# Token gather of a mixture-of-experts kernel: two expert units served by one float32r gather in two parts

## The chip, the cores and the metric

The kernel runs on one core of a Trainium2 chip, in one launch. Its time is the device time in microseconds: three runs gave 1655.13, 1655.5 and 1658.3 us, the median is 1655.5 us. The profile is of one further execution.

## The reference

Two layers, each a token mixer and then a mixture of experts (MoE), on 256 tokens of 1024 channels, all float32. The change lies in the MoE:

```
scores = sigmoid(xf @ w_router)                  # 64 experts
idx    = top 8 of the experts in the 4 best of 8 groups, by scores + b_router
w      = scores[idx] / (sum + 1e-20) * 2.5
y[t]   = sum over the 8 experts e of token t:  w[t,e] * swiglu(x[t], w1[e], w3[e], w2[e])
shared = swiglu(x, ws1, ws3, ws2)
x      = x + g_f * (y + shared)
# swiglu(x, w1, w3, w2) = (silu(x @ w1) * (x @ w3)) @ w2 ; w1, w3: 1024x256, w2: 256x1024
```

Every expert's three matrices (3 MB) are used by every execution, so each layer reads 201 MB of expert weights.

## The kernel before

Names: PE is TensorE (PEld its weight loads), DVE VectorE, ACT ScalarE, SP SyncE, which issues all weight DMAs (SPq in the profile).

**Units.** `moe_body` (L1366) runs 27 units per layer (`UNITS`, L58 to L67): units of 2 experts with 64 token slots each, of 4 experts with 32 slots, and four of 1 expert with 128 slots. The first three units hold the six experts with fixed numbers; the others are sorted by load, so their weights are found by numbers that the routing computes (`ids`, read into registers by SP, L246).

**One unit** (loop at L1613), in PE's order, which is written out by hand:
- `psT<-w,xe`: the up projection. `xe` is the unit's input (128 slots, 1024 channels), w a tile of `w13`.
- `psG<-posTi,identb` and `psG<-wg,oh`: token positions and weights of the slots; DVE makes from them `oT` (scatter one-hots) and `gt`, and `hh`, the gated product (L1626 to L1637).
- `psA<-oT,Y`: `combine` (L1605) scatters the unit before into the accumulators, 16 float32r products of 128x128 by 256 columns.
- two transposes of `hh`, then ACT copies them to `hT_` (L1653).
- `gather(u + 1, 0)`: 4 channel blocks of the next unit's input, `ht` (the tokens, float32) times the one-hot `oh` of 128 columns, two token tiles each.
- `psS<-w,hT_`: `lower` (L1659), the down projection, in two halves; ACT and DVE write `Y` and its remainder (`weigh`, L1675).
- `gather(u + 1, 1)`: the other 4 channel blocks. DVE copies the first half to `xe`, ACT the second.

A float32 product is two instructions on PE, a float32r product one. DVE builds `oh` of the next unit after `gt` (L1579).

**Weights.** `Stream` (L105) issues the loads in the order of use. Tiles are 2 MB; there are nine slots, five named `w` in a ring and four named `wx`, dealt out by `PATTERN` (L70). A unit of 2 experts takes three tiles, of 4 experts six, of 1 expert one and a half. SP waits for a slot to be free, then issues; a slot is free when PE has read its tile for the last time. Loads of experts beyond the first six wait for the routing.

**Routing.** Ahead of the units, `h` is transposed into `ht` (`h_tok`, L1374), DVE computes the routing (L1455 to L1543), and PE fills its waits with the shared expert (`up`, `down`). `gather(0, ...)` follows.

Of the kernel before, what the change touches and what calls it, by code (L numbers as in the profile page):

```python
# [11 lines left out]
F32 = mybir.dt.float32  # L12
F32R = mybir.dt.float32r
BF16 = mybir.dt.bfloat16
I32 = mybir.dt.int32
AF = mybir.ActivationFunctionType
OP = mybir.AluOpType
# [4 lines left out]
P = 128  # L22
D = 1024
KC = D // P
S = 256
NT = S // P
# [35 lines left out]
UNITS = list(_F)  # L62
# [4 lines left out]
NU = len(UNITS)  # L67
# [63 lines left out]

# what a mixer keeps in the extra weight slots until it has no more use for it (tag, floats, buffers)
ROOMS = ((("hp", 1144, 1), ("e0", 385, 1), ("e1", 385, 1), ("e2", 385, 1), ("e3", 385, 1),
# [6 lines left out]
class Shared:  # L140
    """A pool of which some tags lie in the extra weight slots."""

# [26 lines left out]
def trunk(ctx, tc, A, out, dbg=None):  # L169
    nc = tc.nc  # L170
# [20 lines left out]
    def bank(tag):  # L191
        if tag == "S":
            turn[0] ^= 1
            tag = f"S{turn[0]}"
        return ps.tile([P, 512], F32, name="ps" + tag, tag=tag, bufs=4 if tag == "A" else 1)

    def mm(o, lhsT, rhs, start=True, stop=True):
        pe.matmul(out=o, lhsT=lhsT, rhs=rhs, start=start, stop=stop, skip_group_check=True)  # L198

    # ---------------------------------------------------------------- weights  # L200
    st = Stream()
# [112 lines left out]

    # ---------------------------------------------------------------- constants
    tcol = [const.tile([P, NCOL], F32, name=f"tcol{l}") for l in range(L)]
# [124 lines left out]

    # ---------------------------------------------------------------- helpers
    def rsqrt(pool, ss, scale, tags=None, out=None, gap=None):
# [47 lines left out]
    def c2(ap, n=2):  # L491
        return ap.rearrange("p (c t) -> p c t", c=n)

    # ---------------------------------------------------------------- vectors
    modv = [const.tile([P, 48], F32, name=f"modv{l}") for l in range(L)]
# [18 lines left out]

    # ---------------------------------------------------------------- modulation
    mod_ready = set()
# [25 lines left out]

    # ---------------------------------------------------------------- norm
    def chan_sum(b, x, w, first, last):
# [36 lines left out]

    # ---------------------------------------------------------------- mixer
    def mixer(l, before):
# [7 lines left out]
    def mixer_body(l, pool, before=None):  # L591
# [15 lines left out]

        # weights: split into a rounded part and its remainder, ahead of their products
        seq = []
# [113 lines left out]

        # modulation vectors, a few vector operations at a time
        def mod_fill():
# [17 lines left out]

        # convolution
        hp = pool.tile([P, 4, S + 30], F32, name="hp")
# [73 lines left out]

        # rotary embedding and per-head norms  # L820
        def rot(raw):
# [50 lines left out]

        # differential attention
        def a_head(hd):
# [113 lines left out]

        # stick-breaking attention
        def c_head(hd):  # L990
# [100 lines left out]
        def quads(ns):  # L1091
# [5 lines left out]
            if l == 0:  # L1097
                # the first half of the channels in plain float32, ahead of the second half's modulation
                for n in ns:
                    w = wget(("in", n)).rearrange("p (j f) -> p j f", j=KC)  # L1100
                    for c in range(4):
                        for j in range(4):
                            mm(out(n, c), w[:, j, c * P:(c + 1) * P], early[j], start=j == 0 and c % 2 == 0, stop=False)
                second()
# [246 lines left out]

    # ---------------------------------------------------------------- moe
    wscaled = {}
# [12 lines left out]
    def moe_body(l, pool, sums):  # L1366
        st.open.update((l, k) for k in range(NEXTRA))
        st.upto(len(st.items))
        h = pool.tile([P, KC, S], F32, name="h", tag="Y")
        ht = pool.tile([P, NT, KC, P], F32, name="ht")  # L1370
        pre = [pool.tile([P, 1024], F32, name="pre", tag="xe", bufs=2) for _ in range(2)]
        hsT = pool.tile([P, 2, S], F32, name="hsT")

        def h_tok(t, jq):  # L1374
            b = bank("A")
            for k in range(4):
                pe.transpose(out=b[:, k * P:(k + 1) * P], in_=h[:, jq * 4 + k, t * P:(t + 1) * P], identity=ident)
            src = c2(b, 4)
            se.activation(ht[:, t, jq * 4:(jq + 1) * 4], src, AF.Copy)

        with tc.manual_schedule(engines={ET.DVE, ET.Activation}):
            # norm, logits
            w2s = st.get(("s2", l))
            ws2 = w2s[:, 0:2048].rearrange("p (j f) -> p j f", j=2)
            wr = w2s[:, 2048:2048 + KC * NE].rearrange("p (j e) -> p j e", j=KC)
            sq = pre[0][:, 0:S]
            se.activation(sq, xT[:, KC - 1], AF.Square)
# [14 lines left out]
            w13s = st.get(("s13", l)).rearrange("p (j m f) -> p m j f", m=2, j=KC)  # L1402
            # shared expert, in the waits of the routing
            sil = pre[1][:, 512:1024]

# [19 lines left out]
            def some(g, n=99):  # L1425
                for _ in range(n):
                    if next(g, 1):
                        return
# [25 lines left out]

            # routing  # L1455
            bi = pool.tile([P, NT, NE], F32, name="bi", tag="oT", bufs=2)
# [37 lines left out]

            # positions, ranks, permutation
            bp = bank("T")
# [35 lines left out]
            for t in range(NT):  # L1532
                mm(bw[:, P + t * NE:P + (t + 1) * NE], wT[:, t * P:(t + 1) * P], perm)
            some(up_, UP2)
            idt = pool.tile([1, NE], I32, name="idt")
            ve.tensor_copy(idt, bq[0:1, 0:NE])
# [5 lines left out]
            wg = pool.tile([P, NT, NE], F32, name="wg")  # L1542
            ve.tensor_copy(wg, bw[:, P:P + NT * NE].rearrange("p (t e) -> p t e", t=NT))  # L1543

        def overflow_ids():
# [28 lines left out]

        # experts
        oh = {}
        xe = {}

        def onehot(u):  # L1579
            i0, n, c = UNITS[u]  # L1580
            o = oh[u] = pool.tile([P, NT, P], F32, name="oh", bufs=2)
            ve.tensor_tensor(o.rearrange("p t (i c) -> p t i c", c=c),
                             iof[:, None, None, 0:c].to_broadcast([P, NT, n, c]),
                             posI[:, :, i0:i0 + n].unsqueeze(3).to_broadcast([P, NT, n, c]), op=OP.is_equal)
            xe[u] = pool.tile([P, KC, P], F32, name="xe", bufs=2)

        def gather(u, hf):
            b = bank("G" if u else "A")
            for k in range(4):
                for t in range(NT):  # L1590
                    mm(b[:, k * P:(k + 1) * P], ht[:, t, 4 * hf + k], oh[u][:, t], start=(t == 0), stop=(t == NT - 1))
            dst = xe[u][:, 4 * hf:4 * hf + 4]
            if hf:
                se.activation(dst, c2(b, 4), AF.Copy)
            else:
                ve.tensor_copy(dst, c2(b, 4))

        onehot(0)
        for hf in range(2):
            gather(0, hf)  # L1600
        some(up_)
# [11 lines left out]
        for u, (i0, n, c) in enumerate(UNITS):  # L1613
            X = xe[u]
            b = bank("T")
            nj = KC // n
            for j in range(KC):
                if j % nj == 0:
                    wt_ = st.get(("w13", l, i0, j // nj)).rearrange("p (k j f) -> p k j f", k=n, j=nj)
                for k in range(n):  # L1620
                    mm(b[k * c:(k + 1) * c, :], X[:, j, k * c:(k + 1) * c], wt_[:, k, j % nj],
                       start=(j == 0), stop=(j == KC - 1))
# [7 lines left out]
            for t in range(NT):  # L1630
                mm(bg[:, S:S + n], oh[u][:, t], wg[:, t, i0:i0 + n], start=(t == 0), stop=(t == NT - 1))
            oT = pool.tile([P, S], F32R, name="oT", bufs=2)
# [7 lines left out]
            if u == U_OVER:  # L1640
                overflow(l, pool, r, acc, wres, ovi, st.get(("over", l)))
            nxt = u + 1 < NU
            if nxt:
                onehot(u + 1)
            if u == 0:
# [7 lines left out]
            se.activation(hT_, b[:, 0:2 * P].rearrange("p (j s) -> p j s", j=2), AF.Copy)  # L1653
            if nxt:
                gather(u + 1, 0)
            Y = pool.tile([P, 4, 512], F32R, name="Y")
# [24 lines left out]
            if u < NU - 1:  # L1681
                for hf in range(2):
                    lower(hf)
                    weigh(hf)
                if nxt:
                    gather(u + 1, 1)

        # the last unit by halves of the channels, then the residual
        sums = bank("G")
        sq = pool.tile([P, KC, S], F32, name="nsq", tag="ht")  # L1690

# [74 lines left out]

    # ---------------------------------------------------------------- program
    def opening(pool, split):
# [124 lines left out]
```

## Time and profile before

| | us |
|---|---|
| runs, median (lowest to highest) | 1655.5 (1655.13 to 1658.3) |
| the profiled execution, its span from first to last instruction | 1657.0 |
| PE busy | 1617.4 (98%) |
| DVE busy | 748.7 (45%) |
| ACT busy | 469.0 (28%) |
| DMA queue q1, share of 16 engines | 82.5% |

The page gives no time of the profiled execution beside its span; the span lies within the range of the timed runs. PE's granted clock was 0.986 of 2.4 GHz in the mean. Matmuls overlap, so that "mean ns of one" is longer than the step from one to the next; steps are read from the starts in the timeline. The units of layer 0 run from about 349 to 829 us, those of layer 1 from about 1168 to 1650 us.

### The profile page before, as it was taken

The page shows a single profiled execution, that of the slowest core. Times are in us where ns is not written, and L with a number is a line of the kernel's source. Part 1 is how long each engine was busy: PE and PEld are TensorE (multiplying, and loading weights), DVE is VectorE, ACT ScalarE, POOL GpSimd, SP SyncE. Part 2 cuts the span into 40 slices and gives each one's busy share as a digit, 9 for nine tenths or more (in the row PEclk, how much of TensorE's full clock was granted, in tenths as well). Part 3 has the DMA queues.
Part 4 walks back from the last instruction along what each step waited for, and adds up shares of the span by engine and source line. Part 5 has one row for each costly group of instructions (what it writes and reads, how often), then busy time and mean ns, then how long its engine had stood idle before and what let it go on. Part 6 is the DMA issues. An engine that isn't in the chain of part 4 may idle for free. (4 is left out here: it accounts for less than half of the span.)

```text
span 1657.0 us, 27149 instructions
## 1 busy us (share of the span) xinstructions
PE 1617.4 (98%) x10542; PEld 1132.1 (68%) x10542; DVE 748.7 (45%) x1858; ACT 469.0 (28%) x911; POOL 2.9 (0%) x26
## 2 busy tenths in 40 slices
PE   6999999999999999999989999999999999999998
PEld 5999869875555655555578888898655565555654
DVE  8799988642221221212259997554222121221122
ACT  3546724421111111111244355344011111111111
POOL 0000000000000000000000000000000000000000
PEclk9999979999999999999999999999999999999999
DMA  9885319959999999999969744246799999999997
GB/s 379 352 328 206 149 56 363 392 222 344 369 408 421 364 414 415 413 418 413 410 247 365 280 169 153 102 193 246 275 333 396 412 410 372 402 416 416 415 412 286
DMA packets 99205, 544.10 MB, mean 328 GB/s; under 512 B 11136, under 2 KB 11776, under 8 KB 56064
## 3 DMA queue, kind: packets, MB, share of 16 engines
q1 hardware_dynamic: 99072, 542.32, 82.5%
q8 instruction: 85, 1.39, 0.3%
q14 instruction: 48, 0.39, 0.1%
HBM read 541.23 MB, written 1.05 MB: 327 GB/s over the span
## 5 line engine op out<-in xcount | busy, mean ns | idle before, releaser
L1634 DVE TENSOR_SCALAR oT<-psG,slot 128x256 fp32r<-128x256 f32 x54 | 26.1, 484 | 441.9 <-PE psG L198 441.9
L198 PEld LDWEIGHTS psG<-oh,ht 128*128 128x128 f32 x1664 | 194.5, 192 | 40.6 <-DVE Y L1678 36.0
L198 PE MATMUL psT<-w,xe 128*64 128x512 f32 (+2 forms) x1152 | 217.1, 596 | 3.8 <-DMA w<-in_w_dram 3.8
L198 PE MATMUL psA<-hH,WH 128*128 128x256 f32 x696 | 210.7, 303 | 1.1 <-ACT WH L681 1.1
L198 PE MATMUL psG<-oh,ht 128*128 128x128 f32 x1664 | 207.8, 278 | 0.4 <-issue 0.2
L681 ACT ACTIVATE WH<-w 128x512 fp32r<-128x512 f32 (+2 forms) x272 | 147.8, 553 | 203.9 <-PE psA L198 187.7
L198 PE MATMUL psA<-hH,WL 128*128 128x256 f32 x696 | 198.1, 285 | 1.3 <-DVE WL L682 1.3
L198 PE MATMUL psA<-hL,WH 128*128 128x256 f32 x696 | 197.8, 284 | 0.7 <-DVE hL L570 0.7
L682 DVE TENSOR_TENSOR WL<-w,WH 128x512 fp32r<-128x512 f32 (+2 forms) x272 | 157.2, 590 | 58.5 <-ACT WH L681 57.9
L198 PE MATMUL psT<-wx,xe 128*64 128x512 f32 (+2 forms) x896 | 171.5, 594 | 0.0
L198 PEld LDWEIGHTS psT<-w,xe 128*64 128x64 f32 (+2 forms) x1152 | 67.8, 128 | 126.4 <-issue 118.2
L1678 DVE SCALAR_TENSOR_TENSOR Y<-psS,gt,Y 128x512 fp32r<-128x512 f32 x108 | 81.1, 751 | 161.1 <-ACT Y L1677 161.1
L198 PE MATMUL psA<-room,w 128*128 128x256 f32 x592 | 145.2, 389 | 1.1 <-ACT room L573 1.1
L1677 ACT ACTIVATE Y<-psS,gt 128x512 fp32r<-128x512 f32 x108 | 74.4, 689 | 234.4 <-PE psS L198 234.4
L198 PEld LDWEIGHTS psA<-hH,WH 128*128 128x128 f32 x696 | 133.3, 192 | 5.0 <-ACT WH L681 2.7
L198 PEld LDWEIGHTS psA<-hL,WH 128*128 128x128 f32 x696 | 133.3, 191 | 3.0 <-DVE hL L570 0.9
L198 PEld LDWEIGHTS psA<-hH,WL 128*128 128x128 f32 x696 | 133.1, 191 | 2.2 <-DVE WL L682 2.1
L198 PEld LDWEIGHTS psT<-wx,xe 128*64 128x64 f32 (+2 forms) x896 | 54.9, 129 | 97.8 <-issue 95.4
L198 PEld LDWEIGHTS psA<-room,w 128*128 128x128 f32 x592 | 109.6, 194 | 17.3 <-issue 2.9
L1624 ACT ACTIVATE sl<-psT 128x256 f32<-128x256 f32 x54 | 20.8, 385 | 351.9 <-PE psT L198 351.9
L198 PE MATMUL psA<-oT,Y 128*128 128x256 f32 x864 | 115.9, 286 | 0.9 <-ACT Y L1677 0.8
L525 DVE SCALAR_TENSOR_TENSOR w<-w,room 128x1024 f32<-128x1024 f32 x96 | 115.6, 1219 | 1.5 <-DMA w<-in_w_mod_dram 1.4
(576 smaller groups left out, 1885.2 us busy)
## 6 DMA issues: line engine op xcount, KB each, us to landing
w<-in_w_dram SPq DMA_DIRECT2D x108, 1024.0 KB, 15.7
w<-in_w_dram SPq DMA_DIRECT2D x192, 512.0 KB, 10.2
wx<-in_w_dram SPq DMA_DIRECT2D x92, 1024.0 KB, 13.7
wx<-in_w_dram SPq DMA_DIRECT2D x144, 512.0 KB, 10.2
w<-in_w_in_dram SPq DMA_DIRECT2D x56, 1024.0 KB, 8.6
w<-in_w_mod_dram SPq DMA_DIRECT2D x48, 1024.0 KB, 9.3
w<-in_w_out_dram SPq DMA_DIRECT2D x8, 1024.0 KB, 7.9
wx<-in_w_dram SPq DMA_DIRECT2D x4, 2048.0 KB, 16.5
```

Source lines behind the costliest of these rows:

```text
L198: pe.matmul(out=o, lhsT=lhsT, rhs=rhs, start=start, stop=stop, skip_group_check=True)
L525: ve.scalar_tensor_tensor(t[:, j], t[:, j], 1.0, crow, op0=OP.mult, op1=OP.mult, accum_out=modv[l][:, c:c + 1])
L681: se.activation(H[:, j:], src, AF.Copy)
L682: ve.tensor_tensor(Lo[:, j:], src, H[:, j:].bitcast(F32), op=OP.subtract)
L1624: se.activation(sl, b[:, 0:FF], AF.Silu)
L1634: ve.tensor_scalar(oT, bg[:, 0:S], slot[:, k_:k_ + 1], None, op0=OP.is_equal)
L1677: se.activation(Y[:, hf], b, AF.Copy, scale=gt)
L1678: ve.scalar_tensor_tensor(Y[:, 2 + hf], b, gt, Y[:, hf].bitcast(F32), op0=OP.mult, op1=OP.subtract)
```

## The change

The tokens are kept as two float32r tiles, `htH` (rounded, by ACT) and `htL` (the remainder, by DVE in `h_rest`). A one-hot `oh` now has 256 columns, for two units, and `gather(p, s, tag)` fills one input tile `xe` of 256 slots for both, in four pieces of two channel blocks; a block takes four float32r products (two token tiles, `htH` and `htL`). The pieces for the next pair stand in the second unit of a pair only; the 27th unit has a pair of its own, of 128 columns. `oh` and `xe` have one buffer in place of two. One piece of the gather uses the bank `T`. Comments are taken out, and the scratch for DMAs of GpSimd is set to 4096.

```diff
-        ht = pool.tile([P, NT, KC, P], F32, name="ht")
+        htH, htL = (pool.tile([P, NT, KC, P], F32R, name=n) for n in ("htH", "htL"))
+        rests = []
...
-            se.activation(ht[:, t, jq * 4:(jq + 1) * 4], src, AF.Copy)
+            js = slice(jq * 4, (jq + 1) * 4)
+            se.activation(htH[:, t, js], c2(b, 4), AF.Copy)
+            rests.append((htL[:, t, js], c2(b, 4), htH[:, t, js].bitcast(F32)))
+
+        def h_rest(n):
+            for _ in range(n):
+                lo, src, hi = rests.pop(0)
+                ve.tensor_tensor(lo, src, hi, op=OP.subtract)
...
+        twos = [range(u, min(u + 2, NU)) for u in range(0, NU, 2)]
+        def onehot(p):
+            w = len(twos[p]) * P
+            o = oh[p] = pool.tile([P, NT, w], F32R, name="oh")
+            for k, u in enumerate(twos[p]):
...
+            xe[p] = pool.tile([P, KC, w], F32, name="xe")
+        def gather(p, s, tag):
+            w = len(twos[p]) * P
+            m = 512 // w
+            if m * s >= KC:
+                return
+            b = bank(tag)
+            for k in range(m):
+                parts = [(t, x) for t in range(NT) for x in (htH, htL)]
+                for i, (t, x) in enumerate(parts):
+                    mm(b[:, k * w:(k + 1) * w], x[:, t, m * s + k], oh[p][:, t], start=(i == 0), stop=(i == len(parts) - 1))
+            dst = xe[p][:, m * s:m * s + m]
...
             some(up_, UP2)
+            h_rest(2)
             idt = pool.tile([1, NE], I32, name="idt")
...
+            onehot(0)
+            h_rest(2)
...
-        for hf in range(2):
-            gather(0, hf)
+        for s in range(4):
+            gather(0, s, "A")
...
+            turn_ = u == twos[p][-1] and p + 1 < len(twos)
...
-            if nxt:
-                gather(u + 1, 0)
+            if turn_:
+                gather(p + 1, 0, "G")
...
-                for hf in range(2):
-                    lower(hf)
-                    weigh(hf)
-                if nxt:
-                    gather(u + 1, 1)
+                lower(0)
+                weigh(0)
+                if turn_:
+                    gather(p + 1, 1, "G")
+                    gather(p + 1, 2, "T")
+                lower(1)
+                weigh(1)
+                if turn_:
+                    gather(p + 1, 3, "G")
```

PE in layer 0, before: the end of unit 1 (2 experts), from its scatter to the up projection of unit 2.

```order
L198 MATMUL psA<-oT,Y 128x256 x16
L1651 MATMUL psT<-ident,hh 128x128 x2
L198 MATMUL psG<-oh,ht 128x128 x8
L198 MATMUL psS_3849<-w,hT__3836 64x512 x4
L198 MATMUL psS_3850<-w,hT__3836 64x512 x4
L198 MATMUL psG<-oh,ht 128x128 x8
L198 MATMUL psT<-wx,xe 64x512 x16
```

The same place with the change, from the transposes of unit 0 (first of its pair) to the up projection of unit 2; each left-out stretch repeats the pair of `htH` and `htL` (eight products to a piece).

```order
L1668 MATMUL psT<-ident,hh 128x128 x2
L198 MATMUL psS_3744<-wx,hT__3741 64x512 x4
L198 MATMUL psS_3745<-wx,hT__3741 64x512 x4
L198 MATMUL psT<-w,xe 64x512 x16
...
L1668 MATMUL psT<-ident,hh 128x128 x2
L198 MATMUL psG<-oh,htH 128x256
L198 MATMUL psG<-oh,htL 128x256
...
L198 MATMUL psS_3852<-w,hT__3839 64x512 x4
...
L198 MATMUL psT<-oh,htL 128x256
L198 MATMUL psS_3853<-w,hT__3839 64x512 x4
...
L198 MATMUL psT<-wx,xe 64x512 x16
```

Unit 0 now goes from its transposes straight to `psS`; unit 1 gathers for units 2 and 3 in four pieces around the two halves of its `psS`.

DVE in layer 0, before: from the last of the routing to the shared expert's product `hsT`.

```order
L1525 TENSOR_SCALAR posT<-posT 64x256
L1550 SCALAR_TENSOR_TENSOR cap<-cap,cap_3951 64x1
L1551 TENSOR_SCALAR cap_3951<-rank 64x1
L1552 TENSOR_TENSOR cap<-cap,cap_3951 64x1
L1536 CAST idt<-psT 1x64
L1555 TENSOR_SCALAR wres,ov<-posT,cap 64x256
L1539 COPY posI<-psG 128x128
L1541 CAST posTi<-psT 64x256
L1543 COPY wg<-psG 128x128
L1582 TENSOR_TENSOR oh<-iof,posI 128x256 x2
L1556 TENSOR_TENSOR wres<-wres,wT 64x256
L1416 TENSOR_TENSOR hsT<-psS_3582,pre 128x512
```

The same place with the change.

```order
L1561 TENSOR_SCALAR posT<-posT 64x256
L1385 TENSOR_TENSOR htL<-psA,htH 128x512 x2
L1573 CAST idt<-psT 1x64
L1576 COPY posI<-psG 128x128
L1578 CAST posTi<-psT 64x256
L1580 COPY wg<-psG 128x128
L1396 TENSOR_TENSOR oh<-iof,posI 128x2x128 x2
L1385 TENSOR_TENSOR htL<-psA,htH 128x512 x2
L1452 TENSOR_TENSOR hsT<-psS_3582,hsT 128x512
```

Two subtractions stand ahead of `idt` (the expert numbers for SP) and two behind the one-hots; the overflow's `cap` and `wres` moved behind `hsT`.

## Rows read from the trace of the kernel before

**Rows 1.** The page, part 1: busy time, share of the span, instructions.
```profile
span 1657.0 us, 27149 instructions
PE 1617.4 (98%) x10542; PEld 1132.1 (68%) x10542; DVE 748.7 (45%) x1858; ACT 469.0 (28%) x911; POOL 2.9 (0%) x26
```
**Rows 2.** Windows: stretch, its length, busy per engine, PE clock, DMA share, GB/s.
```profile
349.30:460.00 110.70, 109.81 (x700) 64.03 (x702) 22.83 (x54) 15.09 (x28) 0.00 (x0) 1.00 0.93 353
580.00:820.00 240.00, 238.09 (x1603) 133.24 (x1599) 50.61 (x115) 38.03 (x69) 0.20 (x1) 1.00 1.02 414
1166.00:1643.00 477.00, 473.50 (x3057) 271.65 (x3055) 99.01 (x229) 72.31 (x132) 0.00 (x0) 1.00 0.99 392
1166.00:1270.00 104.00, 103.11 (x631) 60.20 (x633) 20.50 (x48) 14.32 (x26) 0.00 (x0) 1.00 0.92 343
1360.00:1390.00 30.00, 30.00 (x177) 17.53 (x178) 6.15 (x12) 5.10 (x9) 0.00 (x0) 1.00 0.95 345
1390.00:1640.00 250.00, 247.39 (x1652) 139.12 (x1648) 51.48 (x117) 38.41 (x70) 0.00 (x0) 0.99 1.02 412
```
**Rows 3.** SP's waits, 1160 to 1260 us: waiter, releaser, total, times, longest.
```profile
SPq L251 <- PE psS L198: 47.7, 5, 24.8
SPq L251 <- PE psT L198: 25.8, 9, 6.0
```
**Rows 4.** Timeline, PE, a unit: start, length, engine, operation, count, [idle before].
```profile
654.64 7.09 PE L198 MATMUL psT<-wx,xe 128*64 128x512 f32 x32
662.36 2.13 PE L198 MATMUL psA<-oT,Y 128*128 128x256 f32 x16
664.32 0.38 PE L1651 MATMUL psT<-ident,hh 128*128 128x128 f32 x2
664.54 1.95 PE L198 MATMUL psG<-oh,ht 128*128 128x128 f32 x16
666.42 3.70 PE L198 MATMUL psS<-w,hT__6091 128*64 128x512 f32 x16
670.05 2.05 PE L198 MATMUL psG<-oh,ht 128*128 128x128 f32 x16
672.03 3.65 PE L198 MATMUL psT<-w,xe 128*64 128x512 f32 x16
```
**Rows 5.** Timeline, PE and SP, the last unit and last load of either layer.
```profile
815.11 0.33 SPq L251 DMA_DIRECT2D wx<-in_w_dram  x1
824.55 1.88 PE L198 MATMUL psS<-wx,hT__7205 128*32 128x512 f32 x4
...
1630.32 4.20 SPq L251 DMA_DIRECT2D wx<-in_w_dram  x4
1643.55 1.95 PE L198 MATMUL psS<-w,hT__14033 128*32 128x512 f32 x16 [0.47 <-ACT hT__14033 L1653]
1645.29 1.88 PE L198 MATMUL psS<-wx,hT__14033 128*32 128x512 f32 x4
```
**Rows 6.** Tile `wx`, 1600 to 1657 us: from issue to landing.
```profile
DMA to landing us min/median/max: 10.2/10.3/13.8
```
**Rows 7.** Timeline: DVE beside the routing and in a unit, PE's first gather.
```profile
345.07 0.21 DVE L1536 CAST idt<-psT 1x64 int32<-1x64 f32 x1 [1.71 <-PE psT L198]
349.11 3.73 PE L198 MATMUL psA<-oh,ht 128*128 128x128 f32 x32
349.31 0.69 DVE L1416 TENSOR_TENSOR hsT<-psS,pre 128x512 f32<-128x512 f32 x1 [1.77 <-PE psS L198]
...
663.61 0.43 DVE L1582 TENSOR_TENSOR oh<-iof,posI 128x256 f32<-128x256 f32 x1
```
**Rows 8.** Timeline, PE: a unit of 1 expert after a wait for its weights.
```profile
1527.95 8.83 PE L198 MATMUL psT<-w,xe 128*128 128x512 f32 x16 [2.23 <-DMA w<-in_w_dram]
```
**Rows 9.** The clock there, in windows, columns as in rows 2.
```profile
1530.00:1540.00 10.00, 10.00 (x41) 5.82 (x40) 1.21 (x4) 0.60 (x2) 0.00 (x0) 0.90 1.00 418
```
**Rows 10.** The chain of work that ended last: start, length, engine and line.
```profile
1546.76 6.87 PE psT L198 x16
```

More of the change, by code (lines that the diff above doesn't have):

```diff
@@ L1369, in moe_body @@
         h = pool.tile([P, KC, S], F32, name="h", tag="Y")
-        ht = pool.tile([P, NT, KC, P], F32, name="ht")
-        pre = [pool.tile([P, 1024], F32, name="pre", tag="xe", bufs=2) for _ in range(2)]
+        htH, htL = (pool.tile([P, NT, KC, P], F32R, name=n) for n in ("htH", "htL"))
         hsT = pool.tile([P, 2, S], F32, name="hsT")
+        rests = []
         def h_tok(t, jq):
@@ L1377, in h_tok @@
                 pe.transpose(out=b[:, k * P:(k + 1) * P], in_=h[:, jq * 4 + k, t * P:(t + 1) * P], identity=ident)
-            src = c2(b, 4)
-            se.activation(ht[:, t, jq * 4:(jq + 1) * 4], src, AF.Copy)
+            js = slice(jq * 4, (jq + 1) * 4)
[5 more added lines that the diff above has]
+                ve.tensor_tensor(lo, src, hi, op=OP.subtract)
+        oh, xe = {}, {}
+        twos = [range(u, min(u + 2, NU)) for u in range(0, NU, 2)]
[3 more added lines that the diff above has]
+            for k, u in enumerate(twos[p]):
+                i0, n, c = UNITS[u]
+                ve.tensor_tensor(o[:, :, k * P:(k + 1) * P].rearrange("p t (i c) -> p t i c", c=c),
+                                 iof[:, None, None, 0:c].to_broadcast([P, NT, n, c]),
+                                 posI[:, :, i0:i0 + n].unsqueeze(3).to_broadcast([P, NT, n, c]), op=OP.is_equal)
+            xe[p] = pool.tile([P, KC, w], F32, name="xe")
[10 more added lines that the diff above has]
+            dst = xe[p][:, m * s:m * s + m]
+            if s % 2:
+                se.activation(dst, c2(b, m), AF.Copy)
+            else:
+                ve.tensor_copy(dst, c2(b, m))
         with tc.manual_schedule(engines={ET.DVE, ET.Activation}):
@@ L1385, in moe_body @@
             wr = w2s[:, 2048:2048 + KC * NE].rearrange("p (j e) -> p j e", j=KC)
-            sq = pre[0][:, 0:S]
+            sq = pool.tile([P, S], F32, name="pre", tag="sl", bufs=2)
             se.activation(sq, xT[:, KC - 1], AF.Square)
@@ L1402, in moe_body @@
             w13s = st.get(("s13", l)).rearrange("p (j m f) -> p m j f", m=2, j=KC)
-            sil = pre[1][:, 512:1024]
+            sil = hsT.rearrange("p c t -> p (c t)")
             def up(m):
@@ L1573, in moe_body @@
         D_(f"rank{l}", rank)
[L1576 to L1598, printed above, removed]
-        for hf in range(2):
-            gather(0, hf)
+        for s in range(4):
+            gather(0, s, "A")
         some(up_)
@@ L1613, in moe_body @@
         for u, (i0, n, c) in enumerate(UNITS):
-            X = xe[u]
+            p, off = u // 2, u % 2 * P
+            X = xe[p]
+            turn_ = u == twos[p][-1] and p + 1 < len(twos)
             b = bank("T")
@@ L1620, in moe_body @@
                 for k in range(n):
-                    mm(b[k * c:(k + 1) * c, :], X[:, j, k * c:(k + 1) * c], wt_[:, k, j % nj],
+                    mm(b[k * c:(k + 1) * c, :], X[:, j, off + k * c:off + (k + 1) * c], wt_[:, k, j % nj],
                        start=(j == 0), stop=(j == KC - 1))
@@ L1630, in moe_body @@
             for t in range(NT):
-                mm(bg[:, S:S + n], oh[u][:, t], wg[:, t, i0:i0 + n], start=(t == 0), stop=(t == NT - 1))
+                mm(bg[:, S:S + n], oh[p][:, t, off:off + P].bitcast(F32), wg[:, t, i0:i0 + n], start=(t == 0), stop=(t == NT - 1))
             oT = pool.tile([P, S], F32R, name="oT", bufs=2)
@@ L1641, in moe_body @@
                 overflow(l, pool, r, acc, wres, ovi, st.get(("over", l)))
-            nxt = u + 1 < NU
-            if nxt:
-                onehot(u + 1)
+            if turn_:
+                onehot(p + 1)
             if u == 0:
@@ L1681, in moe_body @@
             if u < NU - 1:
-                for hf in range(2):
-                    lower(hf)
-                    weigh(hf)
-                if nxt:
-                    gather(u + 1, 1)
+                lower(0)
[5 more added lines that the diff above has]
+                weigh(1)
+                if turn_:
+                    gather(p + 1, 3, "G")
         sums = bank("G")
-        sq = pool.tile([P, KC, S], F32, name="nsq", tag="ht")
+        sq = pool.tile([P, KC, S], F32, name="nsq", tag="htH")
         def residual(m):
@@ L1881 @@
     from concourse.bass_utils import run_bass_kernel_spmd as _run
-    nc = _bacc.Bacc("TRN2", target_bir_lowering=False, num_devices=1)
+    nc = _bacc.Bacc("TRN2", target_bir_lowering=False, num_devices=1, dynamic_dma_scratch_size=4096)
     arrays, args = {}, {}
```

## The prediction

> **What bounds the kernel now.** I read the page first. PE is busy 98% of the span [rows 1], which says that PE is the bound and that less work on PE is less time. That is an average, and the units need another look: the windows with the DMA rate beside PE's busy time [rows 2]. Two things are to be seen there. In the late part of both layers (580 to 820, 1390 to 1640 us) the DMAs move 414 and 412 GB/s over 250 us without a pause, while PE is busy nearly throughout: two resources are full at once. In the first 104 us of layer 1's units they move only 343, in layer 0 353, and behind the units of one expert 345. Who holds them up is told by SP's waits in the early stretch [rows 3]: for PE's reads of the weights, 47.7 us behind psS and 25.8 us behind psT. So early on the queue lacks free slots, which PE hands out; later the slots are there and the transfers themselves are the limit.
>
> How close the two are is seen at the end. The last load of layer 1 is issued at about 1634.5 us (1630.32 and 4.20) [rows 5]; such a load lands after 10.3 us [rows 6], at about 1644.8; PE takes it at 1645.29. In layer 0 it is 815.11 and 10.3, so 825.4, and PE works on it from 824.55 [rows 5]. PE finishes each layer with no margin behind the weights. A shorter PE alone then ends nothing sooner; the last byte must land sooner.
>
> **What the change takes from PE.** One unit, start to start, is 672.03 - 654.64 = 17.39 us [rows 4]. Its two gathers take 666.42 - 664.54 = 1.88 and 672.03 - 670.05 = 1.98 us, 3.86 together, so 7.72 us for a pair. With the change a pair costs 32 float32r products of 128x128 by 256 columns. The nearest row is the scatter, of the same type and shape: 16 in 664.32 - 662.36 = 1.96 us, 0.1225 us each. 32 of them are 3.92 us. Saved so far: 3.80 us a pair. Bounds for one product: half that, if only the columns counted and the scatter were held by something else, and 0.235 us, two of the steps of the present gather (1.88/16 = 0.1175). I take 0.1225, the row that is alike in everything.
>
> Two small terms go the other way. In the first unit of a pair the gather no longer stands between the transposes and psS, and covered there ACT's copy to hT_. Where no gather stands there now, in the last unit, PE waits 0.47 us for it [rows 5]. In the second unit DVE makes two one-hots, 0.43 us each [rows 7], one more than now; the present one is ready at 664.04, and the gather starts at 664.54, so 0.0 to 0.3 us of wait, the larger for units of four experts; I take 0.3. A pair then saves 3.80 - 0.47 - 0.3 = 3.03 us, a unit 1.5, and the 26 units whose successors are gathered for about 39 us a layer. The lone 27th unit has float32r products of 128 columns, for which there is no row: 32 of them at 0.06 to 0.235 us, 2 to 7.5 us against 3.86; I take 0.12 each, no change, and either end is covered by the wait for weights there.
>
> The routing gains four subtractions of 128x512 from PSUM, 0.69 us each by the row of hsT, and both pairs stand in idle time of DVE [rows 7]: two in the 1.71 us ahead of idt, where three small operations have moved away, two in the 1.77 us ahead of hsT. At zero; without the cover 2.8 us a layer, 1.4 of it ahead of idt, which the loads of the sorted experts wait for. The first gather is 32 products in either version: 3.73 us for the group now, 3.92 then, 0.2 us later.
>
> Copies to xe stay at one DVE and one ACT copy per unit in the mean. With one buffer of xe the copies must come behind the pair's last psT; they do, since the pieces stand behind it in PE's order. The third piece sits in the bank T, which the next psT needs: its DVE copy (0.69) has the whole second half of psS (half of 670.05 - 666.42, 1.8 us) and the fourth piece (1.0) to finish. The order of the loads is unchanged. Nothing here adds to PE.
>
> **What arrives at the end.** If all of it arrived, 39 us twice would be 78. It can't: from 1166 to 1643 us the core moves 477 us x 392 GB/s = 187 MB [rows 2], and at 413 GB/s these take 453 us. That floor leaves 24 us a layer. The 24 us are the stretches below the full rate. The first 104 us carry 35.7 MB, which at 413 take 86.4 us: 17.6 us lost. The stretch at 1360 carries 10.35 MB in 30 us where 25.1 would do: 4.9 us lost. The rest is crumbs.
>
> How much comes back depends on how much sooner PE frees slots. The early stretch holds six units (104/17.4), each 1.5 us shorter: 9 of the 17.6 us. The later dip arises because two units of one expert need few bytes and the queue runs full ahead of PE; with PE 1.5 us a unit faster from the start it falls behind less: 3 to 4 of the 4.9. The sum is 12.5 us a layer by which the last byte lands sooner. In both layers the end follows the last load, as shown, so the end moves by the same: 25 us in all. Off go 0.2 us twice for the first gather, and a little for a slow clock: PE will now wait, and after the one long wait of the present trace, 2.23 us, the same 16 instructions took 8.83 us [rows 8] in place of 6.87 [rows 10], with a granted clock of 0.90 of 2.4 GHz in that window [rows 9]. Most such losses lie in time in which PE would wait anyway; of the last unit's, the one wait that isn't followed by slack, I put 1 us. Net 24 us. The profiled span is 1657.0, within the range of the timed runs and 1.5 above their median, so 1655.5 - 24 = 1631.5; I forecast 1631.
>
> The Trainium skill (HBM Reference, Specifications) gives about 425 GB/s for a core that streams alone, and less when both cores of a pair stream. The trace's long stretches stand at 412 to 414, below the first and far above the second. By 425 the floor would be 440 us in place of 453, and the case of a full queue below would be 26 us shorter.
>
> **Rivals.**
> - The queue is full from the first unit on: both dips vanish, 17.6 + 4.9 = 22.5 us a layer, and 1 or 2 more at the end: 1655.5 - 48 = 1607. For it: slots were the early limit. Against: 9 us of earlier slots can't mend 17.6.
> - The early stretch isn't PE's to mend (the fixed experts' tiles hold the slots, and a load needs its 10 us to land anyway): 4 us of the dip and 2 of the early stretch remain, 6 a layer: 1643. For it: the DMA engines' share there is already 0.92 [rows 2].
> - All of PE's saving arrives: 1655.5 - 78 = 1577. It needs 187 MB in 438 us, 427 GB/s; the trace holds no more than 414 over a long stretch.
> - Slower, by the clock. Once PE waits for weights tile after tile, it may stay at 1.2 GHz. A unit at 1.2 GHz takes twice 15.9 us, 32, where its weights take 187 MB/27 at 413, about 17 us: 15 lost a unit. It decides from the point where the loss exceeds the slack, 39 - 12.5 = 26, and the gain, 12.5: some three such units a layer. Four give 4 x 15 - 39 = 21 us a layer, 1697. Against it: a slow PE lets the weights run ahead, the waits end and the clock comes back, as it did by the step of 6.87 us [rows 10]. The Trainium skill (TensorE: Matmul & The Clock Gate, HAM oscillation) describes just such a loop, in which every tile's wait for a DMA returns the clock to half. By that rule the time would be this 1697; the trace so far shows one slow stretch behind one wait, and recovery within the same unit.
> - The product isn't cheaper: at 0.235 us the pair costs 7.5 against 7.72, and the two waits make it 0.5 us longer, 7 us a layer: 1669. Against it stands the scatter, row by row.
>
> **How the numbers follow.** Landing sooner by about 12.5 us (forecast, 1620 to 1639 by itself): 0.70. Full queue: 0.12. Early stretch unmended: 0.10. All of PE's saving: 0.02. Slow clock 0.03, product not cheaper 0.02; 0.01 is left for no change. About 0.2% (3.3 us) is what a measurement of this kernel can tell from none. Faster is then 0.94, same 0.01, slower 0.05. The range reaches from the full queue to the unmended early stretch with the uncertainty of the latter, 1607 to 1643.
>
> **What would show it.** Right: the windows of the first 104 us rise from 343 to about 375 GB/s, those behind the units of one expert to 400 and more, the late ones stay at 412 to 415; the gathers of a pair take about 3.9 us; psT starts to wait for w and wx, some 20 to 25 us a layer, from the middle of the layer on; PE's busy time falls while DMA sets the pace; the last load of layer 1 is issued near 1610. Wrong: late windows well above 415 (more gain), an early stretch that stays near 345 (less), long stretches of the units with a granted clock of 0.5, or a gather piece over 1.5 us.

## The result and the profile after

The changed kernel takes 1632.35 us (median of 4 runs, 1630.8 to 1632.76) where the kernel before took 1656.78 beside it (4 runs, 1655.13 to 1658.3). The ratio is 0.9846, with a 95% interval of 0.9829 to 0.9862: faster, by 24.4 us. The forecast was 1631, in a range of 1607 to 1643.

First the page of the changed kernel, part 1 (busy time, share of the span and instructions of each engine).

```profile
span 1629.1 us, 25483 instructions
PE 1565.4 (96%) x9710; PEld 1050.0 (64%) x9710; DVE 751.1 (46%) x1866; ACT 469.5 (29%) x911; POOL 2.9 (0%) x26
```

Against [rows 1] PE is busy 52 us less, with 832 matmuls fewer, and the span is 27.9 us shorter. DVE has gained 2.4 us. PE's part still reads as nearly full, 96%, but it now holds waits that the records count as work, as the timeline further down shows: by part 5 of the two pages the same psT products with weights are given 388.6 us before and 415.6 now, 27 us more.

The windows tell it by stretch (stretch, its length, busy time of PE, PEld, DVE, ACT and POOL with the number of instructions, granted clock, DMA share, GB/s). The row of 690 to 700 us answers to [rows 9], the others to [rows 2].

```profile
344.90:449.00 104.10, 101.64 (x610) 56.32 (x608) 24.42 (x62) 16.39 (x30) 0.00 (x0) 1.00 0.95 373
460.00:820.00 360.00, 346.50 (x2042) 178.36 (x2041) 79.37 (x186) 61.17 (x115) 0.20 (x1) 0.99 1.02 414
690.00:700.00 10.00, 8.04 (x24) 3.98 (x21) 0.75 (x1) 1.29 (x2) 0.00 (x0) 0.83 1.00 422
...
1152.00:1256.00 104.00, 101.54 (x596) 54.63 (x595) 23.67 (x61) 15.09 (x28) 0.00 (x0) 0.98 0.95 364
1344.00:1374.00 30.00, 29.53 (x188) 15.17 (x188) 7.21 (x16) 5.49 (x10) 0.00 (x0) 1.00 1.03 410
1270.00:1610.00 340.00, 327.62 (x1917) 165.62 (x1915) 70.84 (x160) 53.91 (x98) 0.00 (x0) 0.99 1.02 414
```

The early stretches have risen from 353 and 343 to 373 and 364 GB/s, the dip from 345 to 410, and the late rate, which was 412 to 414, is 414. The 343 of layer 1 is a little low, since its window begins 1.7 us ahead of the first gather. In 104 us from the gather on, the kernel before moved 349:

```profile
1167.70:1271.70 104.00, 103.11 (x639) 59.09 (x637) 20.37 (x46) 14.32 (x26) 0.00 (x0) 1.00 0.93 349
```

The late rate now holds for 360 us of layer 0 and 340 of layer 1; before, the first 120 us of the same stretches moved 396 and 398. Most of the gain is this: the same bytes at the same ceiling, with less time below it.

The layers, from the first gather to the last twelve psS products, take 465.75 us (344.88 to 810.63) and 468.0 us (1152.1 to 1620.1). Before they took 478.4 (349.11 to 827.50) and 480.5 (1167.7 to 1648.2): 12.6 and 12.5 us less. The lines, from PE's timeline before and then from PE's and SP's timelines now ([rows 7] has the gather at 349.11, a fence further down the products at 1620.15):

```profile
827.50 1.93 PE L198 MATMUL psS<-wx,hT__7205 128*32 128x512 f32 x12
...
1167.71 3.73 PE L198 MATMUL psA<-oh,ht 128*128 128x128 f32 x32
...
1648.23 1.93 PE L198 MATMUL psS<-wx,hT__14033 128*32 128x512 f32 x12
```
```profile
344.88 0.47 PE L198 MATMUL psA<-oh,htH 128*128 128x256 f32 x1
...
796.83 4.06 SPq L251 DMA_DIRECT2D wx<-in_w_dram  x4
...
810.63 2.08 PE L198 MATMUL psS<-wx,hT__7199 128*32 128x512 f32 x12
...
1152.10 0.47 PE L198 MATMUL psA<-oh,htH 128*128 128x256 f32 x1
```

The last load of a layer ends its issue, counted from the first gather, at 456.0 us in layer 0 (800.89 - 344.88) and 458.3 in layer 1 (1610.43 - 1152.10). Before it was 466.3 (815.44 - 349.11) and 466.8 (1634.52 - 1167.71) [rows 5]. So the weights come 10.3 and 8.5 us sooner, and the layers end 12.6 and 12.5 us sooner. The other 2.3 and 4.0 us are a lag of PE behind the weights, which the kernel before had and this one has not.

What lies ahead of layer 0's first gather is 4.2 us shorter, and what lies between the layers 1.3 longer; the first is within what the same code shows from run to run (last section), and the second was not traced further.

Next SP's own waits behind the first gather of layer 1, in 103 us of either kernel (waiter, releaser, total us, times, longest): before from 1169 to 1271.7, now from 1153.4 to 1256.1 us.

```profile
SPq L251 <- PE psS L198: 29.8, 5, 7.3
SPq L251 <- PE psT L198: 28.6, 11, 6.0
```
```profile
SPq L251 <- PE psS L198: 29.2, 5, 8.7
SPq L251 <- PE psT L198: 20.9, 11, 6.5
```

The waits for PE's reads were 58.4 us in this stretch and are 50.1. Slots still hold up the queue there, but less. The 73.5 us of [rows 3] can't be compared with this: 24.8 of them are a single wait that ends at the first gather, ahead of the units, and the changed kernel has the same wait there, of 24.9 us.

The pair itself, on PE's timeline (start, length, instruction, count, and in brackets an idle time with its releaser; 27 of the 32 gather products are left out):

```profile
364.51 3.70 PE L198 MATMUL psS<-wx,hT__3741 128*64 128x512 f32 x16 [0.47 <-ACT hT__3741 L1670]
...
377.67 0.38 PE L1668 MATMUL psT<-ident,hh 128*128 128x128 f32 x2
377.87 0.35 PE L198 MATMUL psG<-oh,htH 128*128 128x256 f32 x1
378.06 0.28 PE L198 MATMUL psG<-oh,htL 128*128 128x256 f32 x1
...
378.77 0.28 PE L198 MATMUL psG<-oh,htL 128*128 128x256 f32 x1
378.98 1.94 PE L198 MATMUL psS<-w,hT__3839 128*64 128x512 f32 x8
380.86 0.38 PE L198 MATMUL psG<-oh,htH 128*128 128x256 f32 x1
...
382.93 1.94 PE L198 MATMUL psS<-w,hT__3839 128*64 128x512 f32 x8
384.80 0.38 PE L198 MATMUL psG<-oh,htH 128*128 128x256 f32 x1
...
385.94 7.09 PE L198 MATMUL psT<-wx,xe 128*64 128x512 f32 x32
```

The pieces take 378.98 - 377.87 = 1.11, 382.93 - 380.86 = 2.07 (two of them) and 385.94 - 384.80 = 1.14 us, 4.32 for a pair, against 7.72 for two units in [rows 4]. From 378.06 to 378.77 are six steps of 0.118 us. The first unit of a pair waits 0.47 us for ACT's copy to hT_. In the second unit the gather follows right behind the transposes: it does not wait for the second one-hot.

And where the rest of the saving went, from the timelines of PE, its weight loads (PEld) and SP in layer 0 and at the end of layer 1:

```profile
693.30 8.80 PE L198 MATMUL psT<-w,xe 128*128 128x512 f32 x16 [1.96 <-DMA w<-in_w_dram]
...
1606.37 4.06 SPq L251 DMA_DIRECT2D wx<-in_w_dram  x4
1607.57 0.14 PEld L198 LDWEIGHTS psT<-w,xe 128*32 128x32 f32 x2 [1.14 <-DMA w<-in_w_dram]
1607.57 1.04 PE L198 MATMUL psT<-w,xe 128*32 128x512 f32 x2 [0.23 <-DMA w<-in_w_dram]
1608.85 1.04 PE L198 MATMUL psT<-w,xe 128*32 128x512 f32 x2 [0.23 <-DMA w<-in_w_dram]
1610.12 1.90 PE L198 MATMUL psT<-w,xe 128*32 128x512 f32 x10 [0.23 <-DMA w<-in_w_dram]
...
1620.15 2.04 PE L198 MATMUL psS<-wx,hT__14021 128*32 128x512 f32 x12
```

PE takes psT in steps of 1.27 us (1608.85 - 1607.57, 1610.12 - 1608.85). A piece of a tile, 512 KB, at 414 GB/s takes 1.27 us: PE works at the pace of the transfers. Of each step the brackets on PE show only 0.23 us as idle, since the records of two matmul instructions, 1.04 us, fill the rest; the weight loads in front of them stand idle for 1.14 us, all of it put down to the DMA. So the sum of PE's idle times (8.3 us behind wx and 5.8 behind w in the whole run) understates the wait, and the steps from start to start, or the idle times of PEld, are the views to use.

### The profile page after: what moved, and what is told of

Same layout as the page of the kernel before. It is cut to its first block, busy times and chain, and to the rows that moved or that the text cites. A ratio compares the mean times of both kernels' runs of the same rounds, so it can differ in the third digit from the quotient of the medians.

```text
span 1629.1 us, 25483 instructions
## 1 busy us (share of the span) xinstructions
PE 1565.4 (96%) x9710; PEld 1050.0 (64%) x9710; DVE 751.1 (46%) x1866; ACT 469.5 (29%) x911; POOL 2.9 (0%) x26
## 5 line engine op out<-in xcount | busy, mean ns | idle before, releaser
L198 PE MATMUL psT<-w,xe 128*64 128x512 f32 (+2 forms) x1152 | 229.1, 598 | 5.9 <-DMA w<-in_w_dram 5.8
L198 PE MATMUL psT<-wx,xe 128*64 128x512 f32 (+2 forms) x896 | 186.5, 599 | 8.3 <-DMA wx<-in_w_dram 8.3
L198 PEld LDWEIGHTS psT<-w,xe 128*64 128x64 f32 (+2 forms) x1152 | 73.3, 129 | 142.5 <-issue 121.7
L198 PEld LDWEIGHTS psT<-wx,xe 128*64 128x64 f32 (+2 forms) x896 | 62.2, 130 | 124.4 <-issue 100.3
L198 PEld LDWEIGHTS psA<-oT,Y 128*128 128x128 f32 x864 | 105.7, 189 | 3.6 <-ACT Y L1694 3.4
L760 DVE SCALAR_TENSOR_TENSOR room<-room,tcol,room 128x256 f32<-128x256 f32 x240 | 104.0, 481 | 0.0
```

The source lines that it names most:

```text
L760: ve.scalar_tensor_tensor(yv[:, ch], hp[:, ch, w:w + S], wc, yv[:, ch], op0=OP.mult, op1=OP.add)
```

## The experiments

A question stood behind each: which of the two limits sets the time of which kernel, which part of the change moves it, and what still holds the early stretch. Each was timed in 3 rounds; beside the first four the kernel before took 1657.25 us, beside the others 1657.13.

**Both kernels with a third of the weight traffic of the routed experts taken out.** The edit, in either kernel:

```
-                if i % 2 == 0:
-                    todo.append((("w2", l, i, 0), load_experts, "w2", l, [i, i + 1], 2048, 0))
...
-                for k in range(n // 2):
+                for k in range(n // 2 if i < N_FIXED else 0):
                     todo.append((("w2", l, i, k), load_experts, "w2", l, items, 4096 // n, k))
...
-                    w = st.get(("w2", l, i0, hf)).rearrange("p (k f) -> p k f", k=4)
+                    w = wraw[1].rearrange("p (k f) -> p k f", k=4)
```

> The kernel before, but the sorted experts' w2 is not loaded: the down projection reads the unit's last w13 tile in its place, so a third of the sorted experts' bytes is gone and PE does the same work (the results of those units are other numbers). Theory (before, PE and the weights are nearly level, the weights matter only at a few waits): 1645 to 1654 us, 3 to 10 less than before. Rival (the weights alone set the pace before): some 60 us less a layer, 1540.

> The changed kernel with the same cut in the loads of w2. Theory (the change saves PE 37 to 39 us a layer, of which the transfers let only 12.5 arrive): all of it arrives, 72 to 78 us less than the kernel before with the same cut, so 1570 to 1580. Rival (what is missing from the saving is lost on PE itself, in its waits for copies, in the bank handovers and in a slow clock, whatever the weights do): the gain stays near 25 us, 1620 to 1628.

Measured: the kernel before 1659.62 us, a ratio of 1.0012 (0.9995 to 1.0028); the changed one 1585.08, 0.9567 (0.9534 to 0.9599). The windows of the same stretch, before's variant first and then after's:

```profile
460.00:820.00 360.00, 357.17 (x2322) 202.41 (x2318) 75.98 (x171) 56.71 (x103) 0.20 (x1) 1.00 0.72 269
```
```profile
460.00:820.00 360.00, 350.79 (x2163) 192.02 (x2160) 91.17 (x216) 70.59 (x137) 0.20 (x1) 0.99 0.74 283
```

At 269 GB/s, two thirds of the ceiling, the kernel before is not a microsecond faster. PE alone sets its time, though its DMAs run at their ceiling for half of each layer. The expected gain of 3 to 10 us was a miss. In the changed kernel the same edit gives 47 us: the weights set its time. Its 1585 lie above the 1570 to 1580 expected, by what the first variant failed to gain; between the two variants lie 74.5 us, in the 72 to 78 expected. So the change takes about 75 us from PE's path, and the times that the limits set are about 1657 (PE, before), 1585 (PE, after) and 1632 (the transfers as PE lets them start, after). The 47 us between the last two are what doesn't arrive.

**Only the pairs, in float32** (the changed kernel with one pass over the tokens in place of two; the one-hot's type goes with it):

```
-        htH, htL = (pool.tile([P, NT, KC, P], F32R, name=n) for n in ("htH", "htL"))
+        htH = pool.tile([P, NT, KC, P], F32, name="htH")
...
-                parts = [(t, x) for t in range(NT) for x in (htH, htL)]
+                parts = [(t, x) for t in range(NT) for x in (htH,)]
```

> Only the pairing: one float32 token tile, 256 one-hot columns, the pieces in the second unit of a pair. A pair costs 32 instructions of 256 columns at twice the step of 128 (2 x 0.1175), 7.5 us against 7.72, and 0.47 for the copy to hT_. Theory: the saving comes from the float32r type together with 256 columns, so this is 1652 to 1662, no gain. Rival (fewer one-hots, copies and bank handovers carry the gain): under 1645.

**Only the type, one unit at a time** (the kernel before with the tokens in two float32r parts):

```
-                    mm(b[:, k * P:(k + 1) * P], ht[:, t, 4 * hf + k], oh[u][:, t], start=(t == 0), stop=(t == NT - 1))
+                parts = [(t, x) for t in range(NT) for x in (htH, htL)]
+                for i, (t, x) in enumerate(parts):
+                    mm(b[:, k * P:(k + 1) * P], x[:, t, 4 * hf + k], oh[u][:, t], start=(i == 0), stop=(i == len(parts) - 1))
```

> Only the type: tokens in two float32r parts, but 128 one-hot columns and a gather per unit in the old places. A unit costs 32 products of 128 columns; the lone unit of the changed kernel had them at 0.112 us each, so 3.6 us against 3.86. Theory: 5 to 7 us a layer of PE work, of which a third arrives: 1648 to 1655. Rival (float32r by itself halves the gather, whatever the columns): near the changed kernel, 1632.

Measured: pairs alone 1667.19 us, 1.006 (1.004 to 1.008); the type alone 1656.25, 0.9997 (0.9979 to 1.0014). PE's timeline of the first, then of the second (13 of 16 products left out):

```profile
636.26 1.99 PE L198 MATMUL psG<-oh,htH 128*128 128x256 f32 x8
638.09 1.89 PE L198 MATMUL psT<-oh,htH 128*128 128x256 f32 x8
639.91 1.94 PE L198 MATMUL psS<-w,hT__5634 128*64 128x512 f32 x8
```
```profile
616.87 0.33 PE L198 MATMUL psG<-oh,htH 128*128 128x128 f32 x1
617.04 0.27 PE L198 MATMUL psG<-oh,htL 128*128 128x128 f32 x1
...
618.60 0.28 PE L198 MATMUL psG<-oh,htL 128*128 128x128 f32 x1
618.81 6.66 PE L198 MATMUL psT<-wx,xe 128*64 128x512 f32 x30
```

In float32 a pair's piece takes 638.09 - 636.26 = 1.83 us, so 256 columns cost 0.229 us for each recorded matmul where 128 cost 0.1175: twice the columns, twice the time. In float32r the half gather of one unit takes 618.81 - 616.87 = 1.94, as before (1.88 and 1.98): 0.111 us a product for 128 columns (618.60 - 617.04, 14 steps), and 0.2 us at the handover. Only the two together use what is cheap: from 128 to 256 columns a float32r product goes from 0.111 to 0.118 us. Neither part alone is worth anything, and pairs alone cost 10 us. Of these 10 the wait for hT_ (13 times 0.47 a layer, 12 us) less 13 times 0.3 a layer that the pieces are shorter (1.85, 3.65 and 1.93, so 7.43 against 7.72) explains 5; the rest was not traced. Both expectations were misses, the second narrowly: the type gave none of the 5 to 7 us a layer.

**One weight slot fewer**, to see whether free slots are what the early stretch lacks:

```
-PATTERN = "01ww2www3"
+PATTERN = "01ww2www"
```

> The changed kernel with eight weight slots in place of nine in the expert stage (the fourth of the wx tiles is not dealt out). PE's work and the bytes are the same. Theory (early loads wait for PE to free a slot, then the transfers set the pace to the end): the last byte lands later by one tile, 2.1 MB at 413 GB/s or 5.1 us, per layer: 1632 + 10, 1640 to 1646. Rival (the early stretch is slow for another reason, such as the time of a load to land): 1630 to 1634.

**Only the rounded tokens**, which takes another 16 products from a pair:

```
-                parts = [(t, x) for t in range(NT) for x in (htH, htL)]
+                parts = [(t, x) for t in range(NT) for x in (htH,)]
```

> The changed kernel without the products of htL (the experts see tokens rounded to float32r): half of the gather is gone, 2 us more a pair, 25 us a layer, three quarters as much again as the change took. Theory (late stretches are set by the transfers): only the early stretch of some six units gains, about 1 us each, 3 to 6 us a layer: 1620 to 1627. Rival (PE still sets the pace): 25 us a layer, 1582.

Measured: 1644.08 us, 0.9926 (0.9903 to 0.9948), with the slot gone, and 1622.91, 0.9796 (0.9769 to 0.9824), with half of the products gone. Both as expected, and they bear on each other. One slot less, with nothing changed on PE, costs 11.7 us against the changed kernel. With the products gone, a pair's gather takes 2.46 us (0.67, 1.13 and 0.66), 1.86 less, and of the 48 us that this takes from PE (26 pairs) 9.4 arrive. The windows of that kernel, in the first 80 us of layer 0:

```profile
350.00:370.00 20.00, 19.53 (x96) 10.95 (x94) 3.47 (x10) 2.14 (x4) 0.00 (x0) 1.00 0.97 378
370.00:390.00 20.00, 20.00 (x110) 9.82 (x108) 4.59 (x10) 3.21 (x6) 0.00 (x0) 1.00 0.98 399
390.00:410.00 20.00, 18.63 (x111) 10.41 (x108) 5.04 (x16) 2.52 (x5) 0.00 (x0) 1.00 1.00 375
410.00:430.00 20.00, 19.53 (x105) 9.11 (x104) 4.37 (x9) 4.28 (x8) 0.00 (x0) 1.00 1.03 413
```

The changed kernel moves 344, 383, 357 and 392 GB/s in them. (Its first gather stands at 344.88, that of this kernel and the next two at 346.8 to 350.8, so single rows compare only roughly.) PE's time still counts where it frees slots, and little elsewhere.

**The shared expert's second product moved from unit 0 to unit 17**, into the time in which PE waits for weights:

```
-            if u == 0:
+            if u == 17:
```

(The accumulators that it started are then started by the first combine.)

> The changed kernel with the shared expert's down projection (7 us of PE in unit 0) moved to unit 17, where PE waits for weights anyway. Slots come free up to 7 us sooner in the early stretch, but the tile that holds its weights stays in its slot till unit 17, which costs one slot (5.1 us by the theory of slots). Theory: 1626 to 1632 (gain of 7 against a loss of 5 a layer). Rival (PE work anywhere in the stage counts alike): no change, 1632, or later by the slot alone, 1642.

Measured: 1664.21 us, 1.0048 (1.0033 to 1.0064), 32 us slower than the changed kernel where 0 to 6 faster was expected: a miss. SP's timeline in the early stretch, its waits from 352 to 850 us (behind the first gather, at 350.75 here), and a window:

```profile
376.59 31.11 SPq L251 DMA_DIRECT2D w<-in_w_dram  x6
```
```profile
SPq L251 <- PE psT L198: 56.6, 8, 19.4
SPq L251 <- PE psS L198: 8.4, 2, 8.1
```
```profile
390.00:410.00 20.00, 18.64 (x100) 8.66 (x96) 3.24 (x10) 2.14 (x4) 0.00 (x0) 1.00 0.35 135
```

In the changed kernel no wait for PE behind the first gather is longer than 8.7 us; here layer 0 has one of 19.3, from which the rate from 390 to 410 us falls to 135 GB/s (357 in the changed kernel), and one of 19.4 between 520 and 560. PE reads ws2 at 668 us instead of 357, so its tile stays in its slot for 17 units more. SP issues the loads in one order, so one load that waits for a slot holds back all behind it, and the loss of 32 us is larger than the 11.7 of one slot less. Why the two waits fall where they do was not traced.

**The same with ws2 in a tile of its own**, loaded ahead, so that its slot is free before the routing (room is made by one buffer each for sl and hT_):

```
+        ws2t = pool.tile([P, 2048], F32, name="ws2t")
+        sp.dma_start(ws2t, A["ws2r"][l][:, 0:2048])
...
-            if u == 0:
+            if u == 17:
```

> As e5_late_down, but the shared expert's down weights lie in a tile of their own, loaded ahead of the routing, so that the slot is free before the routing ends (sl and hT_ have one buffer, and the DMA scratch 2048 for the room). Theory: slots come free 7 us sooner and one more tile is loaded ahead; the early stretch of the changed kernel still loses about 10 us a layer against the full rate, and 7 to 10 of them come back: 1612 to 1620. Rival (the early stretch is bound by the time of a load to land): 1628 to 1632.

Measured: 1622.45 us, 0.9799 (0.9758 to 0.9839), 10 us under the changed kernel, the best complete kernel here; 12 to 20 were expected, so it fell short. Its windows, and PE in unit 0:

```profile
350.00:370.00 20.00, 18.56 (x84) 7.18 (x85) 3.27 (x9) 2.74 (x5) 0.00 (x0) 0.91 0.91 374
370.00:390.00 20.00, 20.00 (x116) 10.71 (x114) 4.68 (x10) 3.34 (x6) 0.00 (x0) 1.00 1.01 419
390.00:410.00 20.00, 18.58 (x111) 10.75 (x108) 5.04 (x16) 2.89 (x6) 0.00 (x0) 1.00 1.01 378
410.00:430.00 20.00, 19.47 (x111) 10.03 (x111) 3.92 (x8) 3.37 (x7) 0.00 (x0) 1.00 1.02 394
```
```profile
359.61 0.44 PE L1677 MATMUL psT<-ident,hh 128*128 128x128 f32 x2 [0.91 <-DVE hh L1653]
360.58 5.37 PE L198 MATMUL psS<-wx,hT__3726 128*64 128x512 f32 x16 [0.53 <-ACT hT__3726 L1679]
```

With the slot free the early rates rise, and the miss of the kernel above turns into a gain: the held slot was its cause, not the late products. How much of the 10 us comes from the free slot and how much from the products moved was not separated. Without the shared expert's products in unit 0, PE waits there for DVE and ACT, the granted clock is 0.91, and 16 psS products take 5.37 us in place of 3.70. That is 1.7 us there; what else is short of the expected 12 was not settled.

## Why the prediction was right

- **Two limits, PE early and transfers late.** Right as to stages; wrong as to the step "PE finishes each layer with no margin behind the weights". The four products at 1645.29, which the prediction read, take the first piece of the last tile; the other pieces are taken by the twelve at 1648.23. Before, the last piece landed at about 1644.8 us: PE was 3.4 us behind the weights there, and about 2 us in layer 0 (827.50 against 825.7). Taking weights out gained nothing. After the change that step is true: the last load is issued by 1606.37 + 4.06 = 1610.43, lands about 10.3 us later, at 1620.7, and the twelve products start at 1620.15. That it is issued near 1610, as forecast, owes 4.2 us to the time ahead of layer 0's first gather, which the change didn't set out to touch.
- **A pair saves 3.03 us.** Near. A product steps by 0.118 us (forecast 0.1225), but each piece has some 0.2 us of handover to the products of the other kind, so the pair's gather is 4.32, not 3.92. The wait for hT_ is 0.47, as said. The 0.3 us for the second one-hot is 0 in this pair; in layer 0 two gathers of 13 start 0.5 us behind their transposes, the others 0.1 to 0.25. Net 7.72 - 4.32 - 0.47 = 2.93. The two variants with fewer weights give 74.5 us for the kernel, where 78 were forecast.
- **The lone unit's gather unchanged.** Right: its two halves in layer 0 of the changed kernel take 1.91 and 1.93 us, 3.84 against 3.86.
- **12.5 us of 39 a layer arrive.** Right in the sum, 12.6 and 12.5, but partly by luck. The prediction had the last byte land 12.5 us sooner and the end move by the same; the last loads are issued 10.3 and 8.5 us sooner, and PE's lag behind the weights, which it put at nothing, gave the other 2.3 and 4.0. Of its parts, the early stretch was too large: layer 1's rose from 349 to 364 GB/s, worth about 4 us of the forecast 9 (104 us x 349/364 is 99.7). The dip was too small: at 410 GB/s nearly all of its 4.9 us came back, not 3 to 4.
- **The waits of [rows 3].** Read too large: a third of them, 24.8 of 73.5 us, is one wait ahead of the units, which the change leaves as it is. That the early queue waits for slots is right all the same, as one slot less costs 11.7 us.
- **The floor of the transfers.** Right: the ceiling stayed at 414, which refutes the rival in which all of PE's saving arrives, in this kernel; it did arrive where a third of the bytes was gone.
- **The full queue (1607) and the early stretch unmended (1643).** Both refuted by the windows: neither 414 nor 343 to 353. The experiments place the real kernel between: one slot less is 1644, a freed slot 1622.
- **The slow clock (1697).** Refuted. PE now waits tile after tile, and the granted clock over the late stretches is 0.99. It falls for single units: the psT at 693.30, behind a wait of 1.96 us, takes 8.80 us, with 0.83 in that window, and later tiles run at full clock again. The Trainium skill (TensorE: Matmul & The Clock Gate, HAM oscillation) describes a loop in which the clock returns to half at every tile's wait for a DMA; this trace shows no such loop, but its usual waits, inside steps of 1.27 us, are also shorter than those of the loop described there.
- **The product not cheaper (1669).** Refuted for float32r; it would have been near the truth for float32 (1667).
- **DVE's subtractions at nothing.** Nothing speaks against it: hsT, written beside layer 0's first gather, [rows 7], stands at 345.3 to 351.1 us in the seven profiled executions with the four subtractions and at 348.9 to 349.8 in the three without. It was not measured by itself, and the spread is wider than the 2.8 us in question.
- **Net 24 us** by medians, 24.4. The two profiled executions differ by 27.9, because they fall on either side of their medians.

## What to carry to other kernels

Where an engine and the transfers are both full, take load off each in turn: the resource whose relief gains nothing isn't yet the limit. What a change of the first can bring ends near the limit of the second, and goes further only as far as the first also holds up the second, as PE does here by its slots (9.4 us of another 48). Price a cheaper product in its new shape and type together, since either alone may be worth nothing. In an in-order queue of loads, count how long each tile holds its slot: one held longer costs far more than the work that it was held for.

## What was not expected of the hardware

- A float32r product of 128x128 by 256 columns steps by 0.118 us and one by 128 columns by 0.111; a recorded float32 matmul by 0.229 and 0.1175. What holds the narrow float32r product was not isolated.
- Matmuls that follow the arrival of their weights are recorded with most of the step inside: 1.04 us for two instructions in steps of 1.27 us, with 0.23 us of idle time shown on PE and 1.14 us on its weight loads.
- Layer 0's mixer, whose code is the same, ran from 60 to 80 us with a granted clock of 0.83 in the profiled execution of before and 1.00 in that of after. That is some 3 of the 4.2 us by which the changed kernel's profiled execution reached its first gather sooner (ACT's timelines are 0.2 us apart at 58 us and 3.3 at 70); in the variants of the changed kernel the same place came 2 to 6 us later than there. A difference of this size ahead of the units is no evidence on a change.
